# HGRN mixer: half-block scores join the run of whole-block scores, with keys and queries kept in two states

## The chip, the cores and the metric

The kernel runs on one core of a Trainium2 chip. The metric is the device time of one execution in microseconds; the median of three runs before the change is 1416.65 us (1416.14 to 1416.93). The engines are TensorE (PE, with PEld for its weight loads), VectorE (DVE), ScalarE (ACT), GpSimd (POOL) and SyncE (SP, which issues the DMAs). SBUF is the on-chip memory that the engines read and write, PSUM the banks into which PE writes.

## The reference

The reference is a decoder of two layers over 512 tokens of width 1024. The first layer mixes tokens with Mamba-2, the second with HGRN2; each is followed by a layer norm, a squared-ReLU MLP and a gate. The change lies in the HGRN2 mixer alone, which has 8 heads of 128 channels:

```python
q, fz, v, g = jnp.split(u @ w_in, 4, axis=-1)
log_f = jnp.logaddexp(jnp.log(lb), jnp.log1p(-lb) + jax.nn.log_sigmoid(fz))
k = (1.0 - lb) * jax.nn.sigmoid(-fz)
...
dec = jnp.exp(jnp.where(mask, diff, -jnp.inf))
scores = jnp.einsum('blhk,bshk,blshk->bhls', q_, kk, dec)
o = jnp.einsum('bhls,bshv->blhv', scores, v_) + jnp.einsum('blhk,bhkv->blhv', q_ * jnp.exp(b_), s_prev)
s_new = jnp.exp(b_last)[..., None] * s_prev + jnp.einsum(
    'bshk,bshv->bhkv', kk * jnp.exp(b_last[:, None] - b_), v_)
```

A score of a query l and an earlier key s is a sum over the channels of query times key times the product of all forget gates between s and l, which differs from channel to channel. All is causal.

## The kernel before

Matrix products in the dense parts are made of three matmuls (`mm3`, lines 120 to 122): each float32 operand is split in a high half (hi, a cast by ACT, line 113) and a low half (lo, a subtraction by DVE, line 116). A unit of weights is 128 x 1024: a DMA into `raw`, the cast into `whi` and the subtraction into `wlo`; `whi` and `wlo` have six buffers each, `raw` three. Such full matmuls of 512 columns are called full matmuls below.

In the HGRN stage the heads go in four pairs (`hcore`, once per pair). What a pair does on PE is a chain of short products with work of DVE and ACT between them. To keep PE at work meanwhile, the chain is a generator: at each `yield` it says how many microseconds' worth of background is to be put there, and `fill` takes so many steps of three full matmuls from a list of jobs (`JOBS`): q and f projections of later heads (`qf`), values and gates (`vg`) and the first half of the output projection (`out0`, whose sums are added by DVE at line 935). PE's order is written out by hand in this way (`manual_schedule`); the orders of DVE and ACT come from a scheduler that goes by priorities. The amounts are `FILL` and `STEPS`; the last pair's are multiplied by `LAST`.

The scores of a pair are built by doubling. Tokens stand in chunks of 128, blocks of 32 and levels m = 0 to 4 with halves of 1, 2, 4, 8 and 16 tokens. At a level, keys of a first half are multiplied by the gate product of their second half, queries of a second half by that of their first, so that afterwards keys run to the end of a doubled piece and queries from its start. The names: `kk` is the tile of the keys (cv in the profile, changed in place), `near` (qd) holds for each block of 32 tokens 88 columns: the plain queries, the running queries (`qd`, columns 32 to 63) and queries of pieces further away; `q` (xs) takes the running queries from level 3 on; `f` (sz) holds the gates; `tots` (y) their products; `pcs` (py0, py1) is a PSUM bank per head; `scbs` (scb) the scores within blocks, filled by masked copies on DVE (`keep`, line 996); `scs` (sc) the whole score matrix.

PE has four runs of short matmuls per pair, 128 rows by 32 columns each, four blocks beside each other: at level 0 (88 columns wide), level 2 (56), level 4 (16: the second half of a block against its first half; all line 1015), and the run of whole blocks (32, line 1080), which takes far queries (`far`, lines 1042 and 1043) for blocks two or three apart. After level 4 the eight diagonal pieces are copied into `scs` (line 1066, ACT); after the run of whole blocks twelve pieces of its PSUM bank follow (`settle`, line 1103, ACT). Then the keys are multiplied up to the end of the chunk (lines 1088 and 1089), turned by PE (line 1111), copied to SBUF by ACT (`kt`, btok, line 1113), multiplied with the values (line 1123) and summed to states (line 1127); the output is line 1141 and 1143.

## Time and profile before

| | before |
|---|---|
| median of the runs | 1416.65 us |
| time of the profiled execution | 1416.5 us |
| its span | 1414.7 us |
| PE busy | 1409.0 us, 8061 matmuls |
| DVE busy | 1056.3 us |
| ACT busy | 753.8 us |
| the four pairs' stage, 829 to 1002 us of the span | 173.0 us: PE 172.3 busy, DVE 127.9, ACT 105.2 |
| granted PE clock in that stage | 1.00 |

In a timeline's row stand the start in the span, the duration, the engine, the line, the operation with output and inputs, the shapes and the count of records; a bracket tells how long the engine was idle before it and what released it. In a grouped row stand the total and the mean duration in ns, then the idle time before. A float32 matmul of the short runs makes two records; so a run of 32 matmuls shows x64. A row of the waits shows who waited for whom: total, times, longest.

### The profile page before, as it was taken

The page shows a single profiled execution, that of the slowest core. Times are in us where ns is not written, and L with a number is a line of the kernel's source. Part 1 is how long each engine was busy: PE and PEld are TensorE (multiplying, and loading weights), DVE is VectorE, ACT ScalarE, POOL GpSimd, SP SyncE. Part 2 cuts the span into 40 slices and gives each one's busy share as a digit, 9 for nine tenths or more (in the row PEclk, how much of TensorE's full clock was granted, in tenths as well). Part 3 has the DMA queues.
Part 4 walks back from the last instruction along what each step waited for, and adds up shares of the span by engine and source line. Part 5 has one row for each costly group of instructions (what it writes and reads, how often), then busy time and mean ns, then how long its engine had stood idle before and what let it go on. Part 6 is the DMA issues. An engine that isn't in the chain of part 4 may idle for free.

```text
span 1414.7 us, 20411 instructions
## 1 busy us (share of the span) xinstructions
PE 1409.0 (100%) x8061; PEld 1173.2 (83%) x8061; DVE 1056.3 (75%) x1759; ACT 753.8 (53%) x1134; POOL 1.9 (0%) x12
## 2 busy tenths in 40 slices
PE   9999999999999999999999999999999999999998
PEld 7888888888988888888888888887898888888887
DVE  7989688698876668687986577677785858667873
ACT  6766465573364444545545547655555454544641
POOL 0000000000000000000000000000000000000000
PEclk9999999999999999999999999999999999999999
DMA  8433333234334444444621421222162444434231
GB/s 307 138 118 120 105 119 112 82 105 144 140 120 134 149 146 137 142 141 166 221 75 49 134 91 64 78 86 91 45 239 105 152 145 137 146 134 164 90 119 45
DMA packets 49391, 178.02 MB, mean 126 GB/s; under 512 B 5520, under 2 KB 6288, under 8 KB 49168
## 3 DMA queue, kind: packets, MB, share of 16 engines
q1 hardware_dynamic: 49296, 176.73, 36.1%
q8 instruction: 63, 1.03, 0.3%
q14 instruction: 32, 0.26, 0.1%
HBM read 174.54 MB, written 2.16 MB: 125 GB/s over the span
## 4 chain that ended last, share of the span: by engine, by line
PE 98%; ACT 1%; DVE 1%; issue 0%; DVEq 0%; ACTq 0%
PE pj L120 25%; PE pj L121 25%; PE pj L122 25%; PE py L120 5%; PE py L122 5%; PE py L121 5%; PE py L747 1%; PE pt L238 1%; PE pm L764 1%; PE pm L714 1%; PE py L1015 1%; PE pt L702 1%; PE py L1141 0%; PE py L1143 0%; PE py L1080 0%; PE pm L153 0%
## 5 line engine op out<-in xcount | busy, mean ns | idle before, releaser
L113 ACT CAST whi<-raw 128x1024 fp32r<-128x1024 f32 x222 | 233.0, 1052 | 327.4 <-PE pj L121 237.7
L120 PE MATMUL pj<-b,whi 128*128 128x512 f32 (+1 forms) x1006 | 382.1, 380 | 0.0
L122 PE MATMUL pj<-b,wlo 128*128 128x512 f32 (+1 forms) x1006 | 379.7, 377 | 0.0
L121 PE MATMUL pj<-b,whi 128*128 128x512 f32 (+1 forms) x1006 | 379.5, 377 | 0.0
L116 DVE TENSOR_TENSOR wlo<-raw,whi 128x1024 fp32r<-128x1024 f32 x222 | 270.1, 1220 | 139.8 <-ACT whi L113 134.8
L121 PEld LDWEIGHTS pj<-b,whi 128*128 128x128 f32 x1006 | 189.5, 188 | 33.6 <-issue 0.9
L122 PEld LDWEIGHTS pj<-b,wlo 128*128 128x128 f32 x1006 | 189.4, 188 | 33.8
L120 PEld LDWEIGHTS pj<-b,whi 128*128 128x128 f32 x1006 | 189.5, 188 | 33.6
L122 PE MATMUL pj<-whi,b 128*128 128x512 f32 x544 | 213.4, 392 | 0.0
L120 PE MATMUL pj<-whi,b 128*128 128x512 f32 x536 | 212.9, 397 | 0.0
L121 PE MATMUL pj<-wlo,b 128*128 128x512 f32 x536 | 210.4, 392 | 0.0
L122 PEld LDWEIGHTS pj<-whi,b 128*128 128x128 f32 x544 | 102.2, 188 | 20.9
L120 PEld LDWEIGHTS pj<-whi,b 128*128 128x128 f32 x536 | 100.8, 188 | 20.3 <-ACT b L1162 0.3
L121 PEld LDWEIGHTS pj<-wlo,b 128*128 128x128 f32 x536 | 100.8, 188 | 19.8 <-issue 0.2
L113 ACT CAST whi<-r 128x1024 fp32r<-128x1024 f32 x72 | 75.7, 1053 | 67.7 <-PE pj L122 38.5
L116 DVE TENSOR_TENSOR wlo<-r,whi 128x1024 fp32r<-128x1024 f32 x72 | 87.7, 1220 | 22.5 <-ACT whi L113 21.9
L122 PE MATMUL py<-whi,b 128*128 128x512 f32 (+1 forms) x250 | 97.0, 388 | 0.0
L121 PE MATMUL py<-wlo,b 128*128 128x512 f32 x224 | 87.2, 389 | 0.0
L120 PE MATMUL py<-whi,b 128*128 128x512 f32 x224 | 87.1, 390 | 0.0
L643 DVE SCALAR_TENSOR_TENSOR cv<-pj,cst,cv 128x509 f32<-128x509 f32 (+2 forms) x66 | 48.7, 745 | 10.5 <-ACT cv L640 9.7
L122 PEld LDWEIGHTS py<-whi,b 128*128 128x128 f32 x250 | 46.9, 188 | 9.7
L120 PEld LDWEIGHTS py<-whi,b 128*128 128x128 f32 x224 | 42.0, 188 | 9.1 <-DVE sg L503 0.3
(309 smaller groups left out, 1849.2 us busy)
## 6 DMA issues: line engine op xcount, KB each, us to landing
raw<-in_w SPq DMA_DIRECT2D x112, 512.0 KB, 3.3
r<-in_w SPq DMA_DIRECT2D x64, 512.0 KB, 3.4
raw<-in_wssd SPq DMA_DIRECT2D x36, 512.0 KB, 4.0
a<-csd SPq DMA_DIRECT2D x16, 512.0 KB, 3.7
raw<-in_wso SPq DMA_DIRECT2D x16, 512.0 KB, 3.3
raw<-in_wg SPq DMA_DIRECT2D x16, 512.0 KB, 3.4
raw<-in_whq SPq DMA_DIRECT2D x16, 512.0 KB, 3.3
raw<-in_whvg SPq DMA_DIRECT2D x14, 512.0 KB, 3.3
```

What stands on the lines that cost most here:

```text
L113: nc.scalar.copy(hi[:, :n], f)
L116: nc.vector.tensor_sub(lo[:, :n], f, f32(hi[:, :n]))
L120: nc.tensor.matmul(out, sh, mh, start=start, stop=False, **kw)
L121: nc.tensor.matmul(out, sh, ml, start=False, stop=False, **kw)
L122: nc.tensor.matmul(out, sl, mh, start=False, stop=stop, **kw)
L238: nc.tensor.transpose(pt[:, j * P : (j + 1) * P], src[:, k * P : (k + 1) * P], ident)
L643: nc.vector.scalar_tensor_tensor(cv[:, d:], ps[:, : T - d], convw[:, i, k : k + 1], cv[:, d:], ALU.mult, ALU.add)
L702: nc.tensor.transpose(pt[:, c * P : (c + 1) * P], xs[:, c * P : (c + 1) * P], ident)
L714: nc.tensor.matmul(pst_[:, c * P : (c + 1) * P], btok[:, c, :], xw[:, c].rearrange("p h q -> p (h q)"), start=True, stop=True)
L747: mm = nc.tensor.matmul(yds[0][64 * r : 64 * r + 64, sl], xdt[:, 2 * c + r, :], m[:, r, sl], start=True, stop=True)
L764: mm = nc.tensor.matmul(yo[:, c * P : (c + 1) * P], pv[:, c - 1].rearrange("p h q -> p (h q)"), cm[:, c * P : (c + 1) * P], start=True, st ...
L1015: nc.tensor.matmul(pcs[r][bs, at : at + n], kk[r][:, ts], qs, start=True, stop=True)
```

## The change

The level 4 run (16 columns, line 1015) no longer stands by itself. Its matmuls (now line 1006, in a helper `scores`) stand in front of the whole-block matmuls (line 1077) of the same head, in one run per pair. For that, two states are kept: the keys of level 4 are written into the first 32 columns of `near` (the plain queries there aren't needed any more) while `kk` stays at level 3; the queries of level 4 are written into `q`, while `near` keeps those of level 3. The halves that a product doesn't touch are copied by ACT: lines 1029 and 1033 (256 columns each; before, line 1028 did this once, for the queries at level 3). The far queries move from `near` into the tile of the gates (sz). The keys up to the chunk's end are written back into `kk` (1086, 1087), with one more ACT copy for the last block (1088). The masked copy of level 4 comes after these, and the eight diagonal copies to `scs` (now line 1117) between and behind those of `settle` (1102).

The background is given out in three parts instead of four: after level 1, after level 4 and after the merged run, with `STEPS` of its own for the last pair.

```diff
-STEPS = (2.0, 2.0, 1.4, 1.33)
+STEPS = ((2.2, 2.7, 1.83), (2.55, 2.7, 1.48))
...
+        def scores(r, col, base):
+
+            n = (88 if base == 0 else 64) - col
+            for c in range(NCH):
+                for b in range(0, P, 32):
+                    bs, ts = tokens(c, b)
+                    at, qs = base + n * c, near[r][:, ts.start // 32, col : col + n]
+                    nc.tensor.matmul(pcs[r][bs, at : at + n], kk[r][:, ts], qs, start=True, stop=True)
...
-                nc.vector.tensor_mul(kv[:, :, 0, :], kv[:, :, 0, :], bc(tv[:, :, 1], 2, half))
+                kn = kv if m < 4 else near[r][:, :, :32].rearrange("p b (two u) -> p b two u", two=2)
+                nc.vector.tensor_mul(kn[:, :, 0, :], kv[:, :, 0, :], bc(tv[:, :, 1], 2, half))
...
-                    if m == 3:
-                        nc.scalar.copy(new[:, :, :, 0], old[:, :, :, 0])
-                        qd[r] = q[r]
...
+                    nc.scalar.copy(kn[:, :, 1, :], kv[:, :, 1, :])
+                    old = qd[r].rearrange("p b (two u) -> p b two u", two=2)
+                    qv = q[r].rearrange("p (b two u) -> p b two u", two=2, u=half)
+                    nc.vector.tensor_mul(qv[:, :, 1, :], old[:, :, 1, :], bc(tv[:, :, 0], 2, half))
+                    nc.scalar.copy(qv[:, :, 0, :], old[:, :, 0, :])
+                    qd[r] = q[r]
...
-                far = [t.rearrange("p k l -> p (k l)")[:, : 96 * NCH].rearrange("p (c d u) -> p c d u", c=NCH, u=32) for t in near]
+                far = [t[:, : 96 * NCH].rearrange("p (c d u) -> p c d u", c=NCH, u=32) for t in f]
...
-                elif m == 4:
-                    pc = pc[:, 224:288].rearrange("p (c l) -> p c l", c=NCH)
-                    keep(scb[:, :, 16:], lmask[:, 7, 16:], pc)
-                    for b in range(0, P, 32):
-                        bs = slice(b, b + 32)
-                        nc.scalar.copy(sc[bs, :, bs], scb[bs])
-            if m not in wide:
-                yield FILL[0] * STEPS[m // 2]
+            if m in (1, 4):
+                yield FILL[0] * steps[m // 4]
...
         for r in R:
+            scores(r, 48, 224)
             qv = byblock(qd[r])
...
-                    nc.tensor.matmul(pcs[r][g : g + 32, at : at + 32], kk[r][:, s0 : s0 + 32], qs, start=True, stop=True)
+                    nc.tensor.matmul(pcs[r][g : g + 32, at : at + 32], near[r][:, s0 // 32, :32], qs, start=True, stop=True)
...
+            nc.scalar.copy(kv[:, :, 3], kn[:, :, 3])
...
-        yield FILL[0] * STEPS[3]
+        for r in R:
+            keep(scbs[r][:, :, 16:], lmask[:, 7, 16:], pcs[r][:, 224:288].rearrange("p (c l) -> p c l", c=NCH))
+        yield FILL[0] * steps[2]
...
             settle(1 - r)
+            for b in range(0, P, 32):
+                nc.scalar.copy(scs[r][b : b + 32, :, b : b + 32], scbs[r][b : b + 32])
```

How this stands in the engines' orders, at three places. PE in the first pair, before: the level 4 run of both heads (py is the head's PSUM bank, xs the queries, cv the keys), and behind it the background (its first three matmuls are shown).

```order
L1015 MATMUL py_1185_7007<-xs_6739,cv_6775 32x16 x16
L1015 MATMUL py_1186_7008<-xs_6809,cv_6845 32x16 x16
L120 MATMUL pj_7089<-b_1001_5912,whi_7085 128x512
L121 MATMUL pj_7089<-b_1003_5914,whi_7085 128x512
L122 MATMUL pj_7089<-b_1001_5912,wlo_7087 128x512
```

PE in the first pair, after, where the second head's half of the merged run begins (qd is `near`, sz the far queries):

```order
L1077 MATMUL py_1185_7010<-sz_6772,qd_6897 32x32 x2
L1006 MATMUL py_1186_7011<-qd_6898,cv_6845 32x16 x16
L1077 MATMUL py_1186_7011<-xs_6809,qd_6898 32x32 x4
L1077 MATMUL py_1186_7011<-sz_6842,qd_6898 32x32 x2
L1077 MATMUL py_1186_7011<-xs_6809,qd_6898 32x32
```

The sixteen-column matmuls have moved between whole-block matmuls; no full matmul stands on either side of them any more. Before, 18 full matmuls stood between the two runs; now 36 stand ahead of the merged run in the first three pairs (27 in the last) and 24 (15) behind it.

DVE in the last pair, before, from the two additions of the output projection (L935) to the key products (L1088):

```order
L935 SCALAR_TENSOR_TENSOR acc_99<-acc_99,pj_8746 128x512
L116 TENSOR_TENSOR wlo_9064<-raw_9060,whi_9062 128x1024
L1021 TENSOR_TENSOR cv_8017<-cv_8017,y_8591 128x16x16
L1032 TENSOR_TENSOR xs_7967<-xs_7967,y_8591 128x16x16
L1021 TENSOR_TENSOR cv_8215<-cv_8215,y_8592 128x16x16
L1032 TENSOR_TENSOR xs_8117<-xs_8117,y_8592 128x16x16
L1042 TENSOR_TENSOR qd_8465<-xs_7967,y_8591 128x4x64
L1042 TENSOR_TENSOR qd_8466<-xs_8117,y_8592 128x4x64
L1043 TENSOR_TENSOR qd_8465<-qd_8465,y_8591 128x4x32
L1043 TENSOR_TENSOR qd_8466<-qd_8466,y_8592 128x4x32
L996 COPY_PREDICATED scb_6688<-lmask_6682,py_1361_8680 128x4x16
L996 COPY_PREDICATED scb_6689<-lmask_6682,py_1362_8681 128x4x16
```

DVE in the last pair, after, from the end of the far queries:

```order
L1045 TENSOR_TENSOR sz_8022<-sz_8022,y_8603 128x4x32
L1045 TENSOR_TENSOR sz_8232<-sz_8232,y_8604 128x4x32
L935 SCALAR_TENSOR_TENSOR acc_99<-acc_99,pj_8696 128x512
L935 SCALAR_TENSOR_TENSOR acc_99<-acc_99,pj_8796 128x512
L1086 TENSOR_TENSOR cv_8025<-qd_8477,y_8603 128x4x64
L1087 TENSOR_TENSOR cv_8025<-qd_8477,y_8603 128x4x32
L1086 TENSOR_TENSOR cv_8235<-qd_8478,y_8604 128x4x64
L1087 TENSOR_TENSOR cv_8235<-qd_8478,y_8604 128x4x32
L996 COPY_PREDICATED scb_6688<-lmask_6682,py_1362_8700 128x4x16
L1096 TENSOR_TENSOR xs_8125<-xs_8125,y_8604 128x4x32
L996 COPY_PREDICATED scb_6689<-lmask_6682,py_1363_8701 128x4x16
```

Level 4 follows level 3 without the additions and the split between them; the two additions now stand behind level 4, and the masked copies behind the key products.

ACT in the last pair, before, from the two casts to the copy of the turned keys:

```order
L113 CAST whi_9062<-raw_9060 128x1024
L113 CAST whi_9068<-raw_9066 128x1024
L1066 COPY sc_6686<-scb_6688 32x4x32 x4
L1066 COPY sc_6687<-scb_6689 32x4x32 x4
L1103 COPY sc_6686<-py_1361_8680 32x2x96 x2
L1103 COPY sc_6686<-py_1361_8680 32x2x64
L1103 COPY sc_6687<-py_1362_8681 32x2x96 x2
L1103 COPY sc_6687<-py_1362_8681 32x2x64 x2
L1103 COPY sc_6687<-py_1362_8681 32x2x32 x2
L1103 COPY sc_6686<-py_1361_8680 32x2x64
L1103 COPY sc_6686<-py_1361_8680 32x2x32 x2
L1113 COPY btok_8924<-pt_8920 128x384
```

ACT in the last pair, after, from the copies of each chunk's last block of keys:

```order
L1088 COPY cv_8025<-qd_8477 128x4x32
L1088 COPY cv_8235<-qd_8478 128x4x32
L1117 COPY sc_6686<-scb_6688 32x4x32 x2
L1102 COPY sc_6687<-py_1363_8701 32x2x96 x2
L1102 COPY sc_6687<-py_1363_8701 32x2x64 x2
L1102 COPY sc_6687<-py_1363_8701 32x2x32 x2
L1117 COPY sc_6686<-scb_6688 32x4x32 x2
L1102 COPY sc_6686<-py_1362_8700 32x2x96 x2
L1102 COPY sc_6686<-py_1362_8700 32x2x64 x2
L1102 COPY sc_6686<-py_1362_8700 32x2x32 x2
L1117 COPY sc_6687<-scb_6689 32x4x32 x4
L1114 COPY btok_8932<-pt_8928 128x384
```

The diagonal copies, which stood ahead of the twelve others in one piece, are mixed with them; all wait for the masked copies, which now come after the merged run, and the copy of the turned keys is behind all twenty in both.

More of the change, by code (lines that the diff above doesn't have):

```diff
@@ L997, in hcore @@
         byblock = lambda t: t.rearrange("p (c b u) -> p c b u", c=NCH, u=32)
+        def scores(r, col, base):
[5 more added lines that the diff above has]
+                    nc.tensor.matmul(pcs[r][bs, at : at + n], kk[r][:, ts], qs, start=True, stop=True)
+        steps = STEPS[h0 == 6]
         for m in range(5):
@@ L1003, in hcore @@
                     distant(r, half)
-            for r in R:
-                if m not in wide and m < 4:
-                    continue
-                n = 88 - wide[m] if m in wide else 16
-                for c in range(NCH):
-                    for b in range(0, P, 32):
-                        bs, ts = tokens(c, b)
-                        if m in wide:
-                            at, qs = n * c, near[r][:, ts.start // 32, wide[m] :]
-                        else:
-                            at, qs = 224 + n * c, qd[r][:, ts.start + 16 : ts.stop]
-                        nc.tensor.matmul(pcs[r][bs, at : at + n], kk[r][:, ts], qs, start=True, stop=True)
+            for r in R if m in wide else ():
+                scores(r, wide[m], 0)
             nb = T // (2 * half)
@@ L1020, in hcore @@
                 tv = tot[r].rearrange("p (b two) -> p b two", two=2)
-                nc.vector.tensor_mul(kv[:, :, 0, :], kv[:, :, 0, :], bc(tv[:, :, 1], 2, half))
+                kn = kv if m < 4 else near[r][:, :, :32].rearrange("p b (two u) -> p b two u", two=2)
+                nc.vector.tensor_mul(kn[:, :, 0, :], kv[:, :, 0, :], bc(tv[:, :, 1], 2, half))
                 if m < 4:
                     old = qd[r].rearrange("p k (s two u) -> p k s two u", two=2, u=half)
-                    new = old if m < 3 else q[r].rearrange("p (k s two u) -> p k s two u", k=T // 32, two=2, u=half)
                     ta = tot[r].rearrange("p (k s two) -> p k s two", k=T // 32, two=2)[:, :, :, 0]
-                    nc.vector.tensor_mul(new[:, :, :, 1], old[:, :, :, 1], bc(ta, 3, half))
-                    if m == 3:
-                        nc.scalar.copy(new[:, :, :, 0], old[:, :, :, 0])
-                        qd[r] = q[r]
-                else:
-                    qv = qd[r].rearrange("p (b two u) -> p b two u", two=2, u=half)
-                    nc.vector.tensor_mul(qv[:, :, 1, :], qv[:, :, 1, :], bc(tv[:, :, 0], 2, half))
+                    nc.vector.tensor_mul(old[:, :, :, 1], old[:, :, :, 1], bc(ta, 3, half))
+                else:
+                    nc.scalar.copy(kn[:, :, 1, :], kv[:, :, 1, :])
[4 more added lines that the diff above has]
+                    qd[r] = q[r]
                 nt.append(tots[r][:, toff : toff + nb])
@@ L1044, in hcore @@
             for r in R:
-                sc, scb, pc = scs[r], scbs[r], pcs[r]
+                scb, pc = scbs[r], pcs[r]
                 if m in wide:
@@ L1060, in hcore @@
                     keep(sv[:, :, :, 3], mv[:, m0 + 2, :, 3], pc[:, :, 48:].rearrange("p c (s u) -> p c s u", u=u))
-                elif m == 4:
-                    pc = pc[:, 224:288].rearrange("p (c l) -> p c l", c=NCH)
-                    keep(scb[:, :, 16:], lmask[:, 7, 16:], pc)
-                    for b in range(0, P, 32):
-                        bs = slice(b, b + 32)
-                        nc.scalar.copy(sc[bs, :, bs], scb[bs])
-            if m not in wide:
-                yield FILL[0] * STEPS[m // 2]
+            if m in (1, 4):
+                yield FILL[0] * steps[m // 4]
         row = lambda k, odd: 32 * (3 - k if odd else k)
@@ L1083, in hcore @@
             kv, tv = byblock(kk[r]), tot[r].rearrange("p (c b) -> p c b", c=NCH)
+            kn = near[r][:, :, :32].rearrange("p (c b) u -> p c b u", c=NCH)
             wv = tots[r][:, toff : toff + 2 * NCH].rearrange("p (c b) -> p c b", c=NCH)
@@ L1087, in hcore @@
             nc.vector.tensor_mul(wv[:, :, 0], tv[:, :, 1], wv[:, :, 1])
-            nc.vector.tensor_mul(kv[:, :, :2], kv[:, :, :2], bc(wv, 3, 32))
-            nc.vector.tensor_mul(kv[:, :, 2], kv[:, :, 2], bc(tv[:, :, 3], 2, 32))
+            nc.vector.tensor_mul(kv[:, :, :2], kn[:, :, :2], bc(wv, 3, 32))
+            nc.vector.tensor_mul(kv[:, :, 2], kn[:, :, 2], bc(tv[:, :, 3], 2, 32))
+            nc.scalar.copy(kv[:, :, 3], kn[:, :, 3])
             nc.vector.tensor_mul(nt[r], tv[:, :, 0], wv[:, :, 0])
```

## The prediction

> **What bounds the kernel now.** I read the page's busy times first, then the chain that ended last, then the list of what TensorE (PE) waited for, and last the timelines of PE, VectorE (DVE) and ScalarE (ACT) in the HGRN stage.

> ```profile
> PE 1409.0 (100%) x8061; PEld 1173.2 (83%) x8061; DVE 1056.3 (75%) x1759; ACT 753.8 (53%) x1134; POOL 1.9 (0%) x12
> PE 98%; ACT 1%; DVE 1%; issue 0%; DVEq 0%; ACTq 0%
> PE py L1015 <- DVE qd L990: 0.7, 2, 0.4
> ```

> PE is the bound from end to end, so a microsecond counts only if PE issues its stream later or sooner. The third row is the only wait of PE in the HGRN stage. A busy PE is no proof of a full pace, since one matmul's bar covers the start of the next; so I read starts. PE around the third short run (level 4) of the first pair:

> ```profile
> 836.57 0.39 PE L122 MATMUL pj<-b,wlo 128*128 128x512 f32 x1
> 836.89 0.99 PE L1015 MATMUL py<-qd,cv 128*32 128x56 f32 x64
> 837.81 0.50 PE L120 MATMUL pj<-b,whi 128*128 128x512 f32 x1
> 838.39 0.39 PE L122 MATMUL pj<-b,wlo 128*128 128x512 f32 x1
> ...
> 843.84 0.39 PE L122 MATMUL pj<-b,wlo 128*128 128x512 f32 x1
> 844.16 0.73 PE L1015 MATMUL py<-xs,cv 128*32 128x16 f32 x64
> 844.82 0.50 PE L120 MATMUL pj<-b,whi 128*128 128x512 f32 x1
> 845.16 0.39 PE L121 MATMUL pj<-b,whi 128*128 128x512 f32 x1
> ```

> Between the L122 at 838.39 and that at 843.84 lie 24 steps of full matmuls: 5.45 us, 0.227 each. The run's 64 records (32 matmuls) start 0.32 after the last full matmul, 0.09 over that pace; they take 844.16 to 844.82, 0.66; and the first full matmul behind them takes 0.34 to the next, 0.11 over. So leaving the full stream for a short run and coming back costs 0.20 beside the run itself.

> **The change, part by part.** The number of matmuls and masked copies is the same, and so are the full matmuls in each pair: 27+27+18+18 = 90 before and 30+36+24 = 90 after in the first three, 21+21+15+12 = 69 and 27+27+15 = 69 in the last. SP's and POOL's orders don't change.

> *One run less per pair.* The sixteen-column scores now stand inside the run of whole blocks, with the same kind of tile (128 rows by 32 columns) on both sides. Its own 0.66 stays; one departure and one return go: 4 x 0.20 = 0.8 us. Ends: nothing, if the two kinds pay the same seam inside the merged run; or both whole edges less one pace, 0.32 + 0.34 - 0.23 = 0.43, times 4 = 1.7. I take 0.8, since the run is measured with that seam. [...]

> *The wait in the last pair.* There PE reaches the second run (level 2) too early:

> ```profile
> 973.12 0.39 PE L122 MATMUL pj<-whi,b 128*128 128x512 f32 x1
> 973.81 0.60 PE L1015 MATMUL py<-qd,cv 128*32 128x56 f32 x32 [0.30 <-DVE qd L990]
> 974.82 0.60 PE L1015 MATMUL py<-qd,cv 128*32 128x56 f32 x32 [0.40 <-DVE qd L990]
> 975.35 0.50 PE L120 MATMUL pj<-whi,b 128*128 128x512 f32 x1
> 974.38 0.28 DVE L990 TENSOR_TENSOR qd<-qd,y 128x128 f32<-128x128 f32 x1
> 974.59 0.42 DVE L1021 TENSOR_TENSOR cv<-cv,y 128x256 f32<-128x256 f32 x1
> ```

> From full matmul to full matmul this takes 975.35 - 973.12 = 2.23; the same run undisturbed in the first pair takes 837.81 - 836.57 = 1.24. The wait costs 0.99, more than the 0.7 that is listed as idle (the lower end). Now 27 full matmuls stand ahead of it for 21, so it is due at 973.12 + 6 x 0.227 + 0.32 = 974.80, behind the last L990 (974.66). The 0.99 goes. What is late next is the merged run.

> *Is the merged run fed in time?* It needs all of level 4 with the far queries, which had a run and 18 full matmuls more.

> ```profile
> 837.56 0.42 DVE L1021 TENSOR_TENSOR cv<-cv,y 128x256 f32<-128x256 f32 x1 [0.75 <-PE py L1015]
> 840.93 0.42 DVE L1026 TENSOR_TENSOR xs<-qd,y 128x256 f32<-128x256 f32 x1
> 844.68 0.42 DVE L1021 TENSOR_TENSOR cv<-cv,y 128x256 f32<-128x256 f32 x1 [1.73 <-PE py L1015]
> 847.10 0.35 DVE L996 COPY_PREDICATED scb<-lmask,py 128x64 f32<-128x64 uint8 x2
> ```

> DVE begins 0.67 after the level 2 run's start (837.56 against 836.89), has issued levels 2 and 3 by 841.27 (840.93 plus a step of 0.34), and needs 847.10 - 844.68 = 2.42 for level 4. Its wait of 1.73 for the level 4 run is gone, because level 4 now writes keys and queries elsewhere. So it is ready 0.67 + 3.71 + 2.42 = 6.8 after the run's start; the merged run is due 0.92 + 36 x 0.227 + 0.2 = 9.3 after it in three pairs, and 0.92 + 27 x 0.227 + 0.2 = 7.25 in the last. Margins 2.5 and 0.45: no wait. Four ACT copies (two new, two moved from level 3; 0.41 each by L1028's row below) lie under DVE's 1.35 us of level 4 products where ACT is free. In the last pair ACT has two casts ahead of them, which in the trace before end at 979.08 + 1.06 = 980.14; were they not sooner, the far queries would be some 0.15 late. They wait for full matmuls that now come sooner; I take 0, and 0.15 as the end.

> ```profile
> L1028 ACT COPY xs<-qd 128x256 f32<-128x256 f32 x8 | 3.3, 406 | 13.6 <-DVE qd L1026 13.6
> L1066 ACT COPY sc<-scb 32x128 f32<-32x128 f32 x32 | 9.5, 296 | 7.8 <-DVE scb L996 7.5
> 979.08 1.06 ACT L113 CAST whi<-raw 128x1024 fp32r<-128x1024 f32 x1 [0.30 <-PE pj L122]
> ```

> *The copies behind the run.* The eight diagonal copies to sc (L1066) ran ahead of the run of whole blocks; now they stand behind it, mixed with the twelve of L1103, and the copy of the turned keys (L1113, btok) that PE's state matmul (L1123) needs is queued behind all twenty. In the last pair:

> ```profile
> 978.32 1.44 DVE L935 SCALAR_TENSOR_TENSOR acc<-acc,pj 128x512 f32<-128x512 f32 x2
> 979.68 1.22 DVE L116 TENSOR_TENSOR wlo<-raw,whi 128x1024 fp32r<-128x1024 f32 x1
> 983.27 0.35 DVE L996 COPY_PREDICATED scb<-lmask,py 128x64 f32<-128x64 uint8 x2
> 985.30 0.43 DVE L1088 TENSOR_TENSOR cv<-cv,y 128x256 f32<-128x256 f32 x1
> 986.39 0.28 DVE L1097 TENSOR_TENSOR xs<-xs,y 128x128 f32<-128x128 f32 x1
> 983.53 2.45 ACT L1066 COPY sc<-scb 32x128 f32<-32x128 f32 x8 [3.40 <-DVE scb L996]
> 989.24 0.48 ACT L1113 COPY btok<-pt 128x384 f32<-128x384 f32 x1
> 991.23 0.61 PE L1123 MATMUL pt<-a,btok 128*128 128x128 f32 x4
> ```

> After the change DVE starts level 2 at 974.80 + 0.67 = 975.47 (0.88 later than the 974.59 above). Levels 2 and 3 end at 978.32 + 0.88 = 979.20, level 4 2.42 later at 981.62, two L935 (979.68 - 978.32 = 1.36) at 982.98, the four key products (986.39 - 985.30 = 1.09) at 984.07; then the masked copy, and 0.26 on (983.53 - 983.27) the first ACT copy, 984.33. The twenty take 989.24 - 983.53 = 5.71: btok starts at 990.04 and ends 0.48 later, at 990.52. PE wants it at 991.23 - 0.99 - 0.20 = 990.04. A new wait of 0.5 us. Ends: 0, if ACT gets a few copies done sooner, and 1.0, with the 0.15 above and late releases.

> In the other pairs the cover is as follows.

> ```profile
> 846.97 1.05 ACT L113 CAST whi<-raw 128x1024 fp32r<-128x1024 f32 x1 [4.80 <-PE pj L121]
> 857.14 0.48 ACT L1113 COPY btok<-pt 128x384 f32<-128x384 f32 x1
> 857.83 0.60 PE L1123 MATMUL pt<-a,btok 128*128 128x128 f32 x4
> 901.27 0.49 ACT L1113 COPY btok<-pt 128x384 f32<-128x384 f32 x1
> 904.02 0.39 PE L1123 MATMUL pt<-a,btok 128*128 128x128 f32 x2
> 946.97 0.48 ACT L1113 COPY btok<-pt 128x384 f32<-128x384 f32 x1 [1.03 <-PE pt L1111]
> 949.88 0.39 PE L1123 MATMUL pt<-a,btok 128*128 128x128 f32 x2
> ```

> The margins before are 0.21, 2.26 and 2.43. In the first pair ACT works without a pause from the cast at 846.97 to btok. That cast waits for a full matmul behind the removed run and so comes 0.66 + 0.20 sooner; the two new key copies (128 columns, at most the 0.30 of L1066's row) take 0.6; PE arrives 0.20 sooner: 0.21 + 0.86 - 0.6 - 0.2, about 0.3 left. In the second the first of the twenty comes some 1.4 later (the key products' 1.09 and a masked copy stand ahead), 0.65 left; the third keeps over 1. I take no wait in these three.

> *Hidden at nothing:* the splits L116 that now stand between level 4 and the keys delay low halves by up to 3 us (two splits of 1.22 and a wait); whi and wlo have six buffers each, so PE uses these units later; should that cover fail, up to 3 us would show. The key copy L1088 ends long before the transposes (24 full matmuls, 5.4 us, behind the run). The f tile held longer is wanted again only in the next pair's background.

> Sum: -0.8 - 0.99 + 0.5 = -1.3 us. The profiled execution took 1416.5 (span 1414.7), the median of the runs shown is 1416.65, 0.15 above it: 1416.65 - 1.3 = 1415.3.

> **Rivals.**
> 1. *No new wait in the last pair.* ACT's order there has slack that I don't see: -1.8, 1414.8. With the upper seam of 1.7 as well, -2.7, 1413.9. For it: ACT is 53% busy; against it: the twenty copies stand in one row behind one mask.
> 2. *The seam is not saved*, since every change of the weights' tile inside the merged run costs as much: -0.99 + 0.5, 1416.15. Against it: the run of whole blocks already mixes its sources, at the same pace as the others.
> 3. *Slower: ACT becomes the limit behind the merged run.* If ACT can begin its row (four activations of the next head, 2.45; key copies, 0.6; twenty copies, 5.7; a cast, 1.05; btok, 0.48: 10.3 us) only when the run ends, PE is at L1123 after 24 full matmuls and 3.45 more, 9.1 us, and waits 1.2. In two pairs with the last one's wait doubled this gives 2 x 1.2 + 1.0 - 1.8 = +1.6, 1418.2; in all four 4.8 - 1.8 = +3.0, 1419.6. It decides from a mean wait of 0.45 per pair (1.8/4). For it: the first pair's margin was 0.21 already; against it: the activations are ready before the run.

> **How the numbers follow.** My forecast (near -1.3) has a chance of 0.45, rival 1 0.2, rival 2 with small extra waits 0.24, rival 3 0.11, of which 0.07 in its full form. Less than 0.2% (2.8 us) is what a measurement of this kernel can hardly tell from no change; all cases but the full rival 3 and a still larger gain than rival 1's (0.04) lie within it: faster 0.04, same 0.89, slower 0.07. The range, 1413.9 to 1417.0, holds rivals 1 and 2 and the lighter waits; rival 3 is left out.

> **What would show it.** Right: the merged run with its 0.32 and 0.34 once per pair, four short runs' edges less; no idle time of L1006 for L990 in the last pair; a wait of about 0.5 at L1126 (the new number of L1123) for btok in the last pair alone. Wrong: a wait of L1077 for DVE's far queries or ACT's copies; waits at L1126 in the first two pairs; full matmuls in the merged run's wake at more than 0.227.

## The result and the profile after

The changed kernel takes 1420.87 us (median of 8 runs, 1417.62 to 1422.96) beside 1416.13 for the kernel before (8 runs, 1415.89 to 1416.93): a ratio of 1.0031, 95% interval 1.002 to 1.0041. The prediction said 1415.3. A second measurement (e9 below) gave 1421.51 beside 1416.92, 1.0027 (1.0018 to 1.0037). The profiled execution took 1419.91 (span 1418.1).

The busy times come first, with the row of the instruction queue, which reads the same on the page of before; then the list of what PE waited for.

```profile
PE 1408.8 (99%) x8061; PEld 1173.7 (83%) x8061; DVE 1056.8 (75%) x1759; ACT 757.5 (53%) x1150; POOL 1.9 (0%) x12
...
q8 instruction: 63, 1.03, 0.3%
```

```profile
PE py L1077 <- issue: 3.2, 1, 3.2
PE pm L153 <- PEq L1295: 0.8, 1, 0.8
PE pt L702 <- ACT btok L671: 0.6, 1, 0.6
PE py L592 <- DVE b L167: 0.2, 1, 0.2
PE pj L120 <- issue: 0.2, 1, 0.2
PE pt L1126 <- ACT btok L1114: 0.2, 1, 0.2
```

PE has the same 8061 matmuls. The wait of the last pair (0.7, L1015 for L990) is gone, the forecast wait of L1126 for btok is there, and a row stands on top that nothing in the prediction names: 3.2 us in which L1077, the whole-block matmul of the merged run, waited for nothing that the profile knows ("issue"). It is a single wait, in the second pair. (The rows of L153, L702 and L592 belong to the first stages, ahead of everything that the change touches; such rows stand in the other kernels too.) PE there, and in the first pair for comparison:

```profile
893.38 0.39 PE L122 MATMUL pj<-whi,b 128*128 128x512 f32 x1
893.70 0.45 PE L1006 MATMUL py<-qd,cv 128*32 128x16 f32 x32
...
898.65 0.19 PE L1077 MATMUL py<-sz,qd 128*32 128x32 f32 x1 [3.23 <-issue]
898.85 0.50 PE L120 MATMUL pj<-whi,b 128*128 128x512 f32 x1
899.18 0.40 PE L121 MATMUL pj<-wlo,b 128*128 128x512 f32 x1
```

```profile
847.49 0.39 PE L122 MATMUL pj<-b,wlo 128*128 128x512 f32 x1
847.81 0.45 PE L1006 MATMUL py<-qd,cv 128*32 128x16 f32 x32
...
849.44 0.50 PE L120 MATMUL pj<-b,whi 128*128 128x512 f32 x1
849.78 0.39 PE L121 MATMUL pj<-b,whi 128*128 128x512 f32 x1
```

The same run takes 849.44 - 847.81 = 1.63 us in the first pair and 898.85 - 893.70 = 5.15 in the second. It stops some 0.2 us before its end, with 15 of its 320 instructions left.

The stage as a whole, from the start of the first 88-column run to the first L238 behind the last pair, gives a measure that is free of what lies ahead of it. By pairs, from one 88-column run to the next (starts read from the timelines):

| | pair 1 | pair 2 | pair 3 | last | stage |
|---|---|---|---|---|---|
| before | 46.19 | 45.86 | 45.86 | 43.17 | 181.08 |
| after | 45.89 | 49.09 | 46.16 | 42.40 | 183.54 |

After starts the stage 0.93 later (830.13 for 829.20). That part isn't the change's: a variant of before (e4 below) starts its stage at 830.66, the changed kernel in a second profile (e9) at 829.53, and ahead of the stage the list shows a wait of L702 that differs from profile to profile (0.6 here, 0.2 in before, 0.9 in e4).

**Where PE's instructions come from.** PE issues 8061 matmuls and 8061 weight loads, 16122 instructions; the queue q8 brought 1.03 MB in 63 packets, so one packet holds 16 KB, and at 1.03 MB for 16122 instructions, 64 bytes each (an estimate that takes all of q8's packets for PE's), that is 256 instructions; the stalls below, all at one place modulo 256, bear it out. A float32 matmul of the short runs makes two matmuls and two weight loads, 4 PE instructions. The merged run has 80 matmuls, 320 instructions, in 1.63 us; the longest unbroken run of before, the whole blocks alone, has 48, that is 192. A full matmul is 2 instructions in 0.227 us. So the merged run eats instructions 22 times as fast as the stream around it, and it is longer than a packet. How little lies ahead of PE, the runs below show.

**Theory A**: PE runs out of instructions inside a long run, when the next packet of 256 is asked for too near the run's start. The asking point is the instruction at which PE stands when the next packet is asked for. In the even stream of before and after packets start when PE's count of instructions is at 152 modulo 256 or a little later, and PE stops where it is at 193, one packet further on; so I placed the asking point some 297 instructions ahead of the one that PE then lacks. In the four pairs it lies -17 (ahead of the start), 8, 34 and 85 instructions from the merged run's start. At -17 the slow full matmuls ahead of the run give the fetch time; at 85 only 235 instructions of the run follow, and full matmuls stretch the rest; at 8 the whole stretch is eaten in some 1.5 us (895.22 - 893.70). **Theory B**: the stall belongs to what the merged run reads or writes, or to its place among the weights' loads in the second pair.

### The profile page after: what moved, and what is told of

It reads as the page before. It is cut to its first block, busy times and chain, and to the rows that moved or that the text cites. A ratio compares the mean times of both kernels' runs of the same rounds, so it can differ in the third digit from the quotient of the medians.

```text
span 1418.1 us, 20448 instructions
## 1 busy us (share of the span) xinstructions
PE 1408.8 (99%) x8061; PEld 1173.7 (83%) x8061; DVE 1056.8 (75%) x1759; ACT 757.5 (53%) x1150; POOL 1.9 (0%) x12
## 3 DMA queue, kind: packets, MB, share of 16 engines
q8 instruction: 63, 1.03, 0.3%
## 4 chain that ended last, share of the span: by engine, by line
PE 96%; ACT 1%; DMA 1%; DVE 1%; issue 0%; DVEq 0%; ACTq 0%
PE pj L120 24%; PE pj L121 24%; PE pj L122 24%; PE py L120 5%; PE py L122 5%; PE py L121 5%; PE py L747 1%; PE pt L238 1%; PE pm L764 1%; PE pm L714 1%; PE py L1006 1%; DMA raw<-in_wssd 1%; PE pt L702 1%; PE py L1144 1%; PE py L1146 0%
## 5 line engine op out<-in xcount | busy, mean ns | idle before, releaser
L113 ACT CAST whi<-raw 128x1024 fp32r<-128x1024 f32 x222 | 233.0, 1051 | 334.6 <-PE pj L121 234.8
L120 PE MATMUL pj<-b,whi 128*128 128x512 f32 (+1 forms) x1006 | 382.0, 380 | 0.0
L122 PE MATMUL pj<-b,wlo 128*128 128x512 f32 (+1 forms) x1006 | 379.7, 377 | 0.0
L121 PE MATMUL pj<-b,whi 128*128 128x512 f32 (+1 forms) x1006 | 379.5, 377 | 0.0
L116 DVE TENSOR_TENSOR wlo<-raw,whi 128x1024 fp32r<-128x1024 f32 x222 | 269.9, 1220 | 146.1 <-ACT whi L113 141.3
L122 PEld LDWEIGHTS pj<-b,wlo 128*128 128x128 f32 x1006 | 189.2, 188 | 33.9
L121 PEld LDWEIGHTS pj<-b,whi 128*128 128x128 f32 x1006 | 189.4, 188 | 33.7 <-issue 0.9
L120 PEld LDWEIGHTS pj<-b,whi 128*128 128x128 f32 x1006 | 189.4, 188 | 33.4
L122 PE MATMUL pj<-whi,b 128*128 128x512 f32 x544 | 213.4, 392 | 0.0
L120 PE MATMUL pj<-whi,b 128*128 128x512 f32 x536 | 212.8, 397 | 0.2 <-issue 0.2
L121 PE MATMUL pj<-wlo,b 128*128 128x512 f32 x536 | 210.3, 392 | 0.0
L122 PEld LDWEIGHTS pj<-whi,b 128*128 128x128 f32 x544 | 102.2, 188 | 21.1
L120 PEld LDWEIGHTS pj<-whi,b 128*128 128x128 f32 x536 | 100.8, 188 | 20.8 <-issue 0.6
L121 PEld LDWEIGHTS pj<-wlo,b 128*128 128x128 f32 x536 | 100.8, 188 | 19.9 <-issue 0.2
L113 ACT CAST whi<-r 128x1024 fp32r<-128x1024 f32 x72 | 75.7, 1053 | 67.7 <-PE pj L122 38.6
L116 DVE TENSOR_TENSOR wlo<-r,whi 128x1024 fp32r<-128x1024 f32 x72 | 87.6, 1220 | 23.6 <-ACT whi L113 23.0
L122 PE MATMUL py<-whi,b 128*128 128x512 f32 (+1 forms) x250 | 97.0, 388 | 0.0
L121 PE MATMUL py<-wlo,b 128*128 128x512 f32 x224 | 87.2, 389 | 0.0
L120 PE MATMUL py<-whi,b 128*128 128x512 f32 x224 | 87.1, 390 | 0.0
L122 PEld LDWEIGHTS py<-whi,b 128*128 128x128 f32 x250 | 47.0, 188 | 9.7
L120 PEld LDWEIGHTS py<-whi,b 128*128 128x128 f32 x224 | 42.0, 188 | 9.1 <-DVE sg L503 0.3
```

The costliest lines, as they stand in the source:

```text
L113: nc.scalar.copy(hi[:, :n], f)
L116: nc.vector.tensor_sub(lo[:, :n], f, f32(hi[:, :n]))
L120: nc.tensor.matmul(out, sh, mh, start=start, stop=False, **kw)
L121: nc.tensor.matmul(out, sh, ml, start=False, stop=False, **kw)
L122: nc.tensor.matmul(out, sl, mh, start=False, stop=stop, **kw)
```

## Experiments

The line numbers of padded kernels are 3 higher than those of the changed kernel.

### e1: the changed kernel with 156 more PE instructions ahead of everything

```diff
+        for i in range(39):
+            g = 32 * (i % 4)
+            nc.tensor.matmul(ps[g : g + 32, 256:272], zero.to_broadcast([P, 32]), zero.to_broadcast([P, 16]), start=True, stop=True)
```

They stand with the warm-up matmuls near the program's start, and write columns that nobody reads.

> The changed kernel with 39 more tiny matmuls (32 x 16, 156 PE instructions) among the warm-up matmuls at the start, where PE waits for its first data anyway. Theory A (instruction supply: the merged run's 80 float32 matmuls are 320 PE instructions in 1.7 us, and PE runs dry where a 16 KB fetch of 256 instructions is asked for near the run's start): the places where a fetch is asked for move by 156 instructions, in the four pairs from about -17, 8, 34 and 85 instructions after the run's start to 83, 108, 134 and 185 (counted modulo 256); none is near the start, no pair shows idle time at L1080, the four pairs take 0.8 us less than before the change, the median is about 1415.4 with a spread under 1.5 us. Theory B (a data wait in the second pair that the profile cannot name): the 3.2 us stay in the second pair, median about 1420.9, spread of 5 us.

Measured: 1415.97 (1415.7 to 1416.9, 11 runs) beside 1417.15; ratio 0.9993 (0.9984 to 1.0001). All that PE waited for:

```profile
PE pm L153 <- PEq L1298: 0.8, 1, 0.8
PE pt L705 <- ACT btok L674: 0.6, 1, 0.6
PE pt L1129 <- ACT btok L1117: 0.2, 1, 0.2
```

The idle named issue is gone, from the second pair and from the third. 39 tiny matmuls that do nothing, 850 us ahead of the place, move the kernel from 4.7 us over its before to 1.2 under it (a gain that the interval doesn't separate from none), so the cause is a matter of the position in the instruction stream.

### e2: the same with 76 instructions

The diff is that of e1 with range(19).

> The same with 19 tiny matmuls (76 PE instructions). Theory A: the places become 163, 188, 214 and 9; the second and third pair lose their stall and the last pair gets one of 2 to 4 us in its merged run; median about 1418.5. Theory B: the stall stays in the second pair, and the last has none.

Measured: 1417.32 (1416.82 to 1420.54, 10 runs); ratio 1.0007 (0.9998 to 1.0016). The head of the waits, and PE in the last pair:

```profile
PE py L1080 <- issue: 2.0, 1, 2.0
PE pm L153 <- PEq L1298: 0.8, 1, 0.8
```

```profile
982.05 0.45 PE L1009 MATMUL py<-qd,cv 128*32 128x16 f32 x32
...
985.69 0.22 PE L1080 MATMUL py<-sz,qd 128*32 128x32 f32 x1 [2.00 <-issue]
985.88 0.50 PE L120 MATMUL pj<-whi,b 128*128 128x512 f32 x1
```

The stall has moved to the last pair, where the asking point now lies 9 from the run's start (the others at 163, 188 and 214). The second pair, with the data, the tiles and the loads of the changed kernel, has none: theory B falls. The idle time is at the lower end of the 2 to 4 us expected, and the median lies 1.2 below the expected one.

### e3: the padding on the kernel before

The diff is that of e1, applied to before.

> The kernel before with the 39 tiny matmuls. Both theories: no change, 1416.1 within 0.4 us, since its runs are at most 192 instructions long and the tiny matmuls stand where PE waits for data. If the tiny matmuls cost or gain time themselves, it shows here, up to 1 us.

Measured: 1417.52 (1417.22 to 1418.31, 10 runs); ratio 1.0002 (0.9993 to 1.0011). The padding alone gives nothing; its gain in e1 is the stall that it avoids.

### e4: the last pair's passes alone

```diff
-STEPS = (2.0, 2.0, 1.4, 1.33)
+STEPS = ((2.0, 2.0, 1.4, 1.33), (2.55, 1.75, 1.4, 1.0))
...
+        steps = STEPS[h0 == 6]
```

Before, with 27, 18, 15 and 9 full matmuls in the last pair for 21, 21, 15 and 12; runs and copies untouched.

> The kernel before with only the last pair's background given out otherwise (27, 18, 15 and 9 full matmuls instead of 21, 21, 15 and 12). My step on the wait: PE no longer waits for L990 in the last pair, -0.99 us, median about 1415.1. Rival: the wait is only put off to a later run of that pair, and the median stays at 1416.1.

Measured: 1415.86 (1415.17 to 1417.26, 11 runs); ratio 0.9991 (0.9983 to 1.0). L1015's wait for L990 is gone from the list, and the last pair takes 1010.77 - 968.58 = 42.19 for 43.17: 0.98 less, by one 88-column start and one L238. So this small part of the change is by itself worth most of the 1.24 that the change gains without a stall (e1).

### e5 and e6: the kernel before with a longer run

```diff
+        for i in range(32):
+            g = 32 * (i % 4)
+            nc.tensor.matmul(pcs[0][g : g + 32, 480:496], kk[0][:, g : g + 32], qd[0][:, :16], start=True, stop=True)
         for r in R:
             qv = byblock(qd[r])
```

Dummies directly ahead of the whole blocks, nothing else of the change; e6 has range(16).

> The kernel before, unchanged but for 32 dummy matmuls (32 columns of weights, 16 moving columns, into 16 unused columns of the scores' bank, never read) directly ahead of the run of whole blocks in each pair: that run becomes as long as the merged one, 320 PE instructions for 192, and nothing else of the change is in it. Theory A (PE runs out of instructions inside a long run when the next 256 are asked for near the run's start): the asking point lies 97, -3, -103 (so 153) and 83 instructions from the run's start in the four pairs, so the second pair alone stalls, 1.5 to 3.5 us, with the idle named issue, near the run's end. The dummies themselves cost 32 x 0.0206 (0.66 us for 32 in the trace of before) = 0.66 a pair, 2.6 in all. Sum +4 to +6 us, ratio about 1.0035. Rival B (the stall belongs to something else of the changed run, its two sources of weights or its new order of writes): +2.6 us, ratio 1.0018, and no idle named issue.

> The same with 16 dummies: the run has 256 PE instructions. Theory A: the asking point lies 97, 61, 25 and 19 instructions from the run's start, and the full matmuls behind the run give the rest of the fetch its time (at 19: 237 instructions of run left, then 60 more at 0.114 us each, 8 us in all): no stall, 4 x 0.33 = +1.3 us, ratio 1.0009. Rival C (any run beyond 192 instructions stalls at such a point): an idle named issue of 1 us or more in the third or last pair, ratio 1.002 or more.

Measured for e5: 1419.54 (1418.81 to 1421.13, 11 runs) beside 1416.92; ratio 1.0019 (1.001 to 1.0027). Its first wait, and PE in the second pair:

```profile
PE py L1083 <- issue: 0.8, 1, 0.8
```

```profile
898.50 0.20 PE L1083 MATMUL py<-qd,cv 128*32 128x32 f32 x1
899.48 0.22 PE L1083 MATMUL py<-xs,cv 128*32 128x32 f32 x2 [0.79 <-issue]
```

For e6: 1418.01 (1417.37 to 1418.67, 11 runs); ratio 1.0007 (0.9998 to 1.0016), no idle named issue. In e6 the first three pairs grow by 0.25, 0.24 and 0.22: 16 dummies cost 0.24, less than the 0.33 expected. In e5 they grow by 0.62, 1.51 and 0.48, so the second has 0.96 beside its dummies (1.51 less the mean of the others). A kernel without any of the change's other parts stalls in the pair where it should, once its run has 320 instructions; at 256 it doesn't, although the asking points of two pairs lie at 25 and 19. The size was off: 1.0 for the 1.5 to 3.5 expected. The ratio alone would fit rival B (1.0018); it is the row named issue, in the second pair and nowhere else, that decides.

### e7: the merged run in two halves

```diff
-STEPS = ((2.2, 2.7, 1.83), (2.55, 2.7, 1.48))
+STEPS = ((2.0, 2.2, 1.48, 1.05), (2.25, 2.7, 1.78))
...
                     nc.tensor.matmul(pcs[r][g : g + 32, at : at + 32], near[r][:, s0 // 32, :32], qs, start=True, stop=True)
+            if r == 0 and h0 < 6:
+                yield FILL[0] * steps[3]
```

> The changed kernel with 12 full matmuls (2.7 us) between the two heads' halves of the merged run in the first three pairs (27, 30, 12, 21 full matmuls for 30, 36, 24), and the last pair's passes at 24, 27, 18 for 27, 27, 15; no padding. The asking points lie 1, 26, 52 and 85 instructions from the first half's start. Theory A: no idle named issue in any pair, since 160 instructions and 24 more at the slow pace lie between; one more seam in three pairs, 3 x 0.20 = +0.6; the wait of PE for btok in the last pair (0.37) gone. Against the kernel before: -0.8 - 0.99 + 0.6 + 0.1 = about -1.1 us, ratio 0.9992. Rival B (the cost belongs to what the merged run needs or writes, not to its length): 2 to 3 us of idle stay in one of the halves, ratio 1.001 or more.

Measured: 1416.08 (1415.62 to 1417.5, 11 runs); ratio 0.9996 (0.9987 to 1.0004). All of its waits:

```profile
PE pm L153 <- PEq L1297: 0.8, 1, 0.8
PE py L592 <- DVE b L167: 0.3, 1, 0.3
PE pt L702 <- ACT btok L671: 0.2, 1, 0.2
```

No padding, asking points 1, 26 and 52 from the first half's start, and no stall: 12 full matmuls in the midst give the packet its time (the tightest had landed 1.86 us ahead). But the pairs take 46.26, 45.92 and 45.92, 0.06 or 0.07 more than before: the extra departure and return eat what the merge saves.

### e8: padded, with other passes in the last pair

The diff is that of e1, and 2.25, 2.7, 1.78 for the last pair's steps.

> The changed kernel with the 39 tiny warm-up matmuls of the first experiment (156 PE instructions, so no pair stalls) and the last pair's passes at 24, 27 and 18 full matmuls for 27, 27 and 15. Mine: the wait of the state matmul for the turned keys in the last pair (0.37 us) goes, as 3 x 0.227 = 0.68 us more lie ahead of it, and no wait appears ahead of the merged run; 0.4 us below the first experiment's ratio of 0.9993, so about 0.9990. Rival: the far queries come late instead, because the merged run is due 0.68 sooner (margin reckoned at 0.45): a wait of 0.2 to 0.4 at the merged run for DVE, ratio 0.9993 or above.

Measured: 1416.05 (1415.22 to 1416.87, 11 runs) beside 1416.92; ratio 0.9992 (0.9983 to 1.0001). L1129's wait for btok is gone (from L1115 at 988.11 to L1129 at 990.86: 2.75, what it took in before), and none came ahead of the merged run. Its stage takes 1009.91 - 830.35 = 179.56, against 179.84 in e1 (829.71 to 1009.55): 0.28 less for the 0.4 expected. It is the shortest stage of all kernels here, 1.5 under before's, though its time can't be told from before's.

### e9 and e10: the size of the stall

e9 is the changed kernel as it is; e10 has e1's diff with range(2), 8 instructions.

> The changed kernel as it is, beside the kernel before once more, for the size of the stall: in the first measurement its runs lay between 1417.62 and 1422.96, 5.3 us apart, where the padded one without a stall kept within 1.2. Theory A with a fetch that competes with the weights' transfers: the stall is there in every run and of varying size, so the profile shows an idle named issue of 1 to 4 us in the second pair again, the median lies 2.5 to 5 us above the kernel before and the runs spread over more than 2.5 us. Rival: the stall is a chance event of some runs; then the lowest runs lie about 1.3 us below the kernel before, and the profile may show none.

> The changed kernel with 2 tiny warm-up matmuls (8 PE instructions) for 39, so every later instruction stands 8 places further on. The asking points lie at -25, 0, 26 and 77 instructions from the merged run's start. PE runs dry 297 instructions after the asking point: in the second pair 23 before the run's end (15 before in the changed kernel), in the third 3 behind it, where the changed kernel has 11 full-pace instructions (1.2 us) to spare. Theory A: idle named issue of 1.5 to 4 us in the second pair as in the changed kernel, and of 1 to 2.5 us in the third, where the changed kernel shows 0.2; ratio 1.003 to 1.005. Rival: 8 instructions make no difference, the third pair stays at 0.2 to 0.5.

Measured for e9: 1421.51 (1419.1 to 1423.24, 11 runs), ratio 1.0027 (1.0018 to 1.0037). The stall is there again, 2.9 us idle in the second pair and 0.6 in the third. But the second pair takes 927.04 - 875.48 = 51.56, 5.7 over before, far more than its idle time. The windows around the stall (columns: PE, weight loads, DVE, ACT, POOL, then the granted clock of PE, the DMA share and GB/s), and the stream behind it:

```profile
892.80:894.70 1.90, 1.90 (x154) 1.55 (x154) 1.48 (x5) 0.40 (x2) 0.00 (x0) 1.00 0.75 235
894.70:897.80 3.10, 0.18 (x12) 0.07 (x8) 0.99 (x5) 1.69 (x6) 0.00 (x0) 0.88 0.56 197
897.80:903.40 5.60, 5.58 (x21) 4.36 (x21) 3.68 (x10) 3.96 (x15) 0.00 (x0) 0.50 0.02 4
```

```profile
898.68 0.63 PE L121 MATMUL pj<-wlo,b 128*128 128x512 f32 x1
899.11 0.63 PE L122 MATMUL pj<-whi,b 128*128 128x512 f32 x1
...
903.38 0.62 PE L120 MATMUL pj<-whi,b 128*128 128x512 f32 x1
...
904.07 0.40 PE L122 MATMUL pj<-whi,b 128*128 128x512 f32 x1
904.31 0.40 PE L120 MATMUL pj<-whi,b 128*128 128x512 f32 x1
```

Here the granted clock falls with the idle time: to 0.50 towards the end of the stall, where it stays for 6.8 us; a full matmul takes 0.427 (11 steps from 898.68 to 903.38) for 0.227. From 898.09 to 903.38 lie 12 steps, 5.29 us for 2.72, so 2.6 us lost: 3.1 of stall and 2.6 of slow clock make the 5.7. In the changed kernel's first profile the same windows show 1.00:

```profile
895.30:898.60 3.30, 0.12 (x9) 0.01 (x1) 0.92 (x5) 1.63 (x6) 0.00 (x0) 1.00 0.53 159
898.60:904.20 5.60, 5.55 (x31) 4.58 (x31) 3.64 (x10) 4.78 (x16) 0.00 (x0) 1.00 0.01 4
```

So a part of the changed kernel's spread comes from the clock. Of e9's 11 runs the three with a mean clock of 0.997 took 1422.07 to 1423.24, the four at 1.000 1419.1 to 1420.2; in the first measurement the two at 0.997 took 1422.13 and 1422.96. A mean of 0.999 tells nothing: e4 and e8, which have no stall, show it in three runs each, and so does the fastest run of the changed kernel, 1417.62. The rest of the spread isn't explained by the runs. Even e9's lowest run lies 2.2 over before's median, where a stall that some runs escape would have left it about 1.3 below. The changed kernel's first profile, at 1419.91 and 1.000, lies 1.0 under its median and before's 0.4 over its own; that is why the medians lie 4.7 apart while the spans differ by 3.4.

In the clock records of the traces the lowered stretches last 6.83 us (e9) and 3.41 (e10), and the full stretch ahead of e9's takes 890.88; these are 2, 1 and 261 steps of 3.413 us, and the full stretches in before (1409.70) and in the changed kernel's first profile (1413.12) are 413 and 414. The length of the gap doesn't tell whether the clock falls: from the start of one matmul to that of the next, the clock fell with a gap of 3.1 us here and of 2.1 in e10, and stayed up with one of 3.4 in the first profile.

Measured for e10: 1419.34 (1417.3 to 1420.92, 11 runs), ratio 1.0015 (1.0006 to 1.0024). The head of its waits, and windows behind the third pair's run:

```profile
PE pj L122 <- issue: 1.7, 1, 1.7
PE py L1080 <- issue: 1.0, 1, 1.0
```

```profile
942.40:944.50 2.10, 0.43 (x3) 0.04 (x1) 2.10 (x8) 2.03 (x8) 0.00 (x0) 1.00 0.01 4
944.50:946.00 1.50, 1.50 (x6) 1.17 (x7) 1.50 (x6) 1.43 (x7) 0.00 (x0) 0.80 0.00 0
946.00:948.00 2.00, 2.00 (x6) 1.61 (x5) 0.45 (x2) 1.91 (x8) 0.00 (x0) 0.50 0.03 8
```

Eight instructions move the third pair's idle time from 0.2 (0.6 in e9) to 1.7, inside the range expected, because the short matmuls now reach up to the point where PE runs dry. The second pair's fell to 1.0, below its range, and so did the ratio.

### All stalls side by side

The instruction at which PE ran dry is counted from the program's start in the order of the records, PE's semaphore instructions included (126 in the changed kernel); the idle time goes from the start of the last matmul to that of the next, so it is some tenths of a us longer than in the lists of waits; packet times are those of the instruction queue in the trace.

| kernel, pair | PE stops at instruction | modulo 256 | PE idle (us) | packet starts, takes | PE goes on |
|---|---|---|---|---|---|
| after, 2 | 10177 | 193 | 895.22 to 898.65 | 895.70, 1.56 | 1.39 behind it |
| after, 3 | 11201 | 193 | 945.75 to 946.36 | 944.14, 0.97 | 1.25 |
| e2, last | 12225 | 193 | 983.50 to 985.69 | 983.32, 1.07 | 1.30 |
| e5, 2 | 10433 | 193 | 898.50 to 899.48 | 896.84, 1.16 | 1.48 |
| e9, 2 | 10177 | 193 | 894.68 to 897.82 | 895.15, 1.44 | 1.23 |
| e9, 3 | 11201 | 193 | 947.70 to 948.74 | 946.49, 0.96 | 1.29 |
| e10, 2 | 10177 | 193 | 895.00 to 896.16 | 893.36, 1.23 | 1.57 |
| e10, 3 | 11201 | 193 | 942.40 to 944.47 | 942.18, 0.98 | 1.31 |

Eight stalls in five executions, all at the same place modulo 256, and PE goes on 1.2 to 1.6 us after the packet has landed. The places without a stall bear this out: the twelve profiles have 180 packets between them in this stretch (15 each), and by their order the other 172 had all landed 1.8 us or more before PE came to their place (1.83 in e5's third pair, 1.86 in e7's). What sets the packet's start isn't settled: by the same count it begins between 0.15 us ahead of the asking point (e10, second pair) and 2.0 behind it. I took the weights' transfers for the cause; they don't sort the cases. In e2's stall nothing else was on the DMA engines from 981 to 987:

```profile
DMA  0000000000000004000000000000000000000000
...
q8 instruction: 1, 0.02, 1.1%
```

and yet PE was idle there for 2.2 us, while e10's shorter stall in the second pair fell among weights.

## Why the prediction was wrong

It was wrong in direction: forecast 1.3 us faster, measured 4.7 slower. The terms of its sum hold up; what failed is a term that it didn't have.

- *One run less per pair, -0.8.* Right in size, a little high. With no stall (e1) the pairs take 45.95, 45.82 and 45.63, less than before by 0.24, 0.04 and 0.23: 0.17 a pair for 0.20. The edges of the merged run are the forecast 0.32 (847.49 to 847.81) and 0.34 (849.44 to 849.78). Rival 2 falls; e7, which puts an edge back, loses the gain again.
- *The wait in the last pair, -0.99.* Right: the passes alone give 0.98 (e4). In the changed kernel the second run follows its full matmul without a wait:

```profile
978.65 0.39 PE L122 MATMUL pj<-whi,b 128*128 128x512 f32 x1
978.97 0.99 PE L1006 MATMUL py<-qd,cv 128*32 128x56 f32 x64
979.89 0.50 PE L120 MATMUL pj<-whi,b 128*128 128x512 f32 x1
```

- *A new wait for btok in the last pair, +0.5.* Right in place and mechanism, 0.37 in size:

```profile
991.41 0.49 PE L1112 MATMUL pt<-cst,cv 128*128 128x128 f32 x3
...
994.53 0.71 PE L1126 MATMUL pt<-a,btok 128*128 128x128 f32 x4 [0.21 <-ACT btok L1114]
```

and ACT, whose copy ends behind all twenty others:

```profile
994.00 0.48 ACT L1114 COPY btok<-pt 128x384 f32<-128x384 f32 x1
```

  3.12 from the transposes to the state matmul, 2.75 where nothing waits (e8). The waiting matmul happens to stand at 193 modulo 256 as well, but its packet had landed 5.9 us before, and in e1, where it stands at 93, the same stretch takes 3.10. It shows in the last pair alone, as forecast, so rival 1 falls, and rival 3 too: ACT's copies are no limit in the other pairs.
- *The sum, -1.3.* With the stall padded away, the stage takes 179.84 for 181.08: -1.24.
- *"Is the merged run fed in time?", margins of 2.5 and 0.45, "no wait".* This is the step that failed. It asked when keys and far queries are ready, and for those the margins held. It didn't ask whether PE's own instructions are there. The term for the removed run also took the merged run's length for granted, the sum of its two parts at their own pace. A row of before's page had the means for the question: the instruction queue's packets, beside PE's count of instructions. Two short runs of 128 and 192 instructions, with 36 slow instructions between them, had each stayed under the 256 of a packet; joined they make 320. No rival had this, and the slower side was given 0.07, all of it for ACT.
- *Its price.* In the profiled execution 49.09 - 45.82 = 3.27 in the second pair and 46.16 - 45.63 = 0.53 in the third, against the same pairs of e1: 3.8 in place of 0. In some executions the lowered clock comes on top, 2.6 in e9's second pair; mean clocks of 0.997 or 0.998, which no kernel without a stall shows, stand in three of the first eight runs and four of e9's eleven. And -1.24 + 3.8 + 0.93 (ahead of the stage) = +3.5, the 3.4 by which the spans differ.

What stays open: how long the packet waits before it starts, and with it whether a stall costs 1 us or 3; and what decides whether the clock falls. Where the gap lies among the steps of 3.41 us doesn't settle it either, by an estimate that counts them from the edges in the clock records: e10's gap, inside one step, left it 1.7 us idle and the clock fell, the first profile's left one 1.8 us idle and it didn't.

## What to carry to other kernels

Count a run of short matmuls in PE instructions (here 4 for each float32 matmul, 64 bytes each) and compare it with the 256 of one instruction packet: no run of 192 stalled here and none of the four of 256 (e6), a run of 320 did, by up to 3.4 us, where the asking point lay between 3 ahead of the run's start and 34 behind it. Break such a run with some 12 full matmuls (in e7 the tightest packet was there 1.9 us ahead, where 1.6 meant a stall), or weigh its length against the 0.2 us that a merge saves; padding works too (e1), but a later edit ahead of the run shifts the boundary again (in e10 8 instructions brought the third pair's idle time from 0.2 to 1.7). The wait named "issue" on the engine that bounds the kernel was not noise here: it stood at instruction 10177 in both profiles of the changed kernel and moved to the last pair when 76 instructions were added near the program's start (e2); it was the instruction supply.
